# A margin behind the modelled landing of transfers, in the planner that orders the engines' queues of a two-layer decoder trunk

## The chip, the cores and the metric

One NeuronCore of one Trainium2 chip runs the kernel; the other cores idle. The metric is the device time of one execution in microseconds (us), and less is better.

## The reference

The input x is 256 positions by 2048 channels, float32, and passes through two layers. What each layer computes, cut to what matters here:

```python
h = rms_norm(x, mix_norm[l])
proj = h @ w_in[l]                       # 2048 -> 1024 + 512 + 2048 + 4096
q, k, v, uv, gate_logits = split(proj)
branch_a = sliding_window_attention(q, k, v, sinks[l]) @ w_attn_branch[l]
branch_b = chunked_sgu(gelu(uv), w_spatial[l], ...) @ w_sgu_branch[l]
x = x + (gates_a * branch_a + gates_b * branch_b) @ w_out[l]
h2 = rms_norm(x, ffn_norm[l])
x = x + (silu(h2 @ w_gate[l]) * (h2 @ w_up[l])) @ w_down[l]     # 2048 -> 5632 -> 2048
```

All is float32, and nearly all of the work is matrix products of the 256 positions with some 470 MB of weights, each weight read once.

## The kernel before

**Products.** A float32 product is made of three single-pass products: each operand is split into a high part and a low remainder. The weights arrive from HBM in tiles `raw` of 128x2x512 floats (512 KB). For each, ScalarE (ACT) writes the high part `whi` (line 520) and VectorE (DVE) the remainder `wlo` (line 521); TensorE (PE) then runs whi·uh, wlo·uh and whi·ul (lines 617 and 618) into PSUM tiles `acc`. The activations' parts are `uh` and `ul`. `raw` has 5 buffers (and four single ones, `k11` to `k22`), `whi` and `wlo` 4 each.

**Paired columns.** Where two 512-column blocks are computed together, a part of the product uses a seven-product scheme. Its entries P1 to P7 take differences of weight tiles, made in place on VectorE (`raw<-raw,raw`, line 506), and of activations (`sums`, split into `sh` and `sl`). In the middle of a pair, partial sums are saved and added (`kept`, lines 644 and 647) and put back into PSUM (`acc<-kept`, lines 645 and 650). P4 starts to write the PSUM tile that the second `kept` of line 647 reads, so PE waits there for that `kept`.

**Activations for the next product.** A result (a chunk of x after the residual, `hid`, a merged branch) is transposed in two steps: VectorE transposes 32x32 blocks into `box` (line 691), and 16 small DMAs, issued by POOL or SP, gather them into `tt` (line 697). ScalarE then reads `tt` and writes `uh` (line 716, or 720 where a norm's scale is applied) or a whole copy `flat` (line 761), and VectorE writes `ul` (lines 717 and 725).

**What sets the order.** PE's instructions stand in the order in which the program writes them. The queues of the other four (DVE, ACT, POOL, SP) are ordered by a planner (`in_order`) that runs while the kernel is built. `works` finds dependencies; `count_back` gives each instruction a due time from PE's order and a table of costs; `play` then plays the program forward by modelled costs. Whenever an engine is free, `play` gives it, of the instructions that are ready at that modelled time, the one that is due first. A transfer's modelled end is a queue of service times plus 1550 to 3100 ns, and the transfer's readers become ready then. The order that comes out is fixed: each engine takes its instructions in turn, and one that must wait holds up all behind it. The lines of `play` at which the change takes effect:

```python
            for u in w.users:
                if (todo[u].engine == w.engine and not w.dma) == (kind == 2):
                    release(u, t + (LATE if w.dma and kind == 1 else 0))
```

Here `w` is an instruction that has just ended in the model, `w.dma` tells that it is a transfer, and `release` makes the reader `u` ready.

Of the kernel before, what the change touches and what calls it, by code (L numbers as in the profile page):

```python
# [17 lines left out]
COST_PE = {"psg": 500, "po": 450, "psc": 400}  # L18
TABLES = {"Exp": 0, "Gelu_apprx_tanh": 11, "Silu": 18}
SWITCH = 4000  # L20
LATE = 0
EARLY = 40000
SPARE = 30000

# [213 lines left out]
def play(todo, users, homes):  # L238
# [9 lines left out]
    def release(k, at):  # L248
        left[k] -= 1
        ready[k] = max(ready[k], at, todo[k].due - EARLY)  # L250
        if not left[k]:
            waiting[todo[k].engine].append(k)
            heappush(events, (ready[k], 0, k))
# [10 lines left out]
    while events:  # L264
        t, kind, k = heappop(events)
        w = todo[k]
        if kind:
# [3 lines that stand above are left out]
        if kind == 1:  # L271
# [1116 lines left out]
```

## Time and profile before

| | us |
|---|---|
| runs of the kernel before (median of 3) | 2458.6 (2449.66 to 2458.63) |
| the profiled execution's own time | 2451.39 |
| its span, first to last instruction | 2449.7 |
| PE busy | 2417.1 (99%) |
| DVE busy | 2106.4 (86%) |
| ACT busy | 1543.6 (63%) |
| mean granted TensorE clock | 0.998 |

In the profile's views L506 is line 506 of the kernel, `out<-in` names the tiles that an instruction writes and reads, and x6 counts equal instructions in a row. In rows of the timeline the two numbers ahead are the start and the length in us, and the bracket gives the engine's idle time before the instruction and what ended it. PE's matmuls overlap: one of 512 columns is shown as 390 ns long, while in steady work the next starts 227 ns after it.

### The profile page before, as it was taken

The numbers are of one execution on the slowest core, as the hardware profiler recorded it, in microseconds if no ns is written. First come the engines' busy times: TensorE is split into PE (matmuls) and PEld (weight loads), VectorE is DVE, ScalarE is ACT, GpSimd is POOL, SyncE is SP. The second block draws the span as 40 slices with busy tenths as digits, with TensorE's granted clock in tenths as the row PEclk, the third lists the DMA queues.
The fourth block names the chain that finished last, engine by engine and source line by source line (L and its number), as shares of the span: only waits on it lengthen the run. The fifth ranks groups of instructions, "written<-read, shape, count | busy, mean of one in ns | idle before, by whom it ended". The sixth has DMA issues, their size and how long they took to land.

```text
span 2449.7 us, 31107 instructions
## 1 busy us (share of the span) xinstructions
PE 2417.1 (99%) x10692; PEld 1973.3 (81%) x10692; DVE 2106.4 (86%) x2409; ACT 1543.6 (63%) x1936; POOL 319.3 (13%) x573
## 2 busy tenths in 40 slices
PE   9999999989999999999999999999999999999999
PEld 7877888868887888888788778887788888887887
DVE  7789777978999898789887987878889999998898
ACT  6477555555666666666665775555666666666665
POOL 1100001122110011002301000011311101110110
PEclk9999999999999999999999999999999999999999
DMA  7855787677578767866767557767776786678664
GB/s 250 259 165 163 190 214 222 225 226 247 168 250 238 214 189 223 263 201 197 246 224 244 173 173 192 207 210 247 228 229 204 221 259 201 201 234 244 203 219 145
DMA packets 287375, 527.17 MB, mean 215 GB/s; under 512 B 28464, under 2 KB 40336, under 8 KB 287216
## 3 DMA queue, kind: packets, MB, share of 16 engines
q1 hardware_dynamic: 263056, 486.36, 64.3%
q0 software_dynamic: 23840, 38.56, 6.1%
q8 instruction: 83, 1.36, 0.2%
q14 instruction: 76, 0.62, 0.1%
q10 hardware_dynamic: 320, 0.27, 0.0%
HBM read 483.66 MB, written 16.78 MB: 204 GB/s over the span
## 4 chain that ended last, share of the span: by engine, by line
PE 56%; DVE 7%; DMA 6%; issue 3%; ACT 1%; POOL 1%; SPq 0%; ACTq 0%; DVEq 0%; POOLq 0%
PE acc L617 37%; PE acc L618 18%; DVE wlo L521 4%; DMA tt<-box 2%; DMA raw<-in_w_down_dram 2%; ACT whi L520 1%; DVE raw L506 1%; DMA raw<-in_w_up_dram 1%; POOL tt L697 1%; DMA raw<-in_w_out_dram 0%; DMA held_x<-part 0%; DVE box L691 0%; PE psc L1061 0%; DVE hid L1327 0%; DMA held_x<-x 0%
## 5 line engine op out<-in xcount | busy, mean ns | idle before, releaser
L520 ACT ACTIVATE whi<-raw 128x1024 fp32r<-128x1024 f32 (+1 forms) x1116 | 1173.4, 1058 | 675.2 <-PE acc L618 530.8
L521 DVE TENSOR_TENSOR wlo<-raw,whi 128x1024 fp32r<-128x1024 f32 (+1 forms) x1117 | 1337.9, 1217 | 241.7 <-ACT whi L520 234.9
L617 PE MATMUL acc<-wlo,uh 128*128 128x512 f32 x2854 | 1116.9, 391 | 17.5 <-DVE kept L647 11.0
L617 PE MATMUL acc<-whi,uh 128*128 128x512 f32 x2854 | 1118.9, 392 | 0.1
L618 PE MATMUL acc<-whi,ul 128*128 128x512 f32 x2854 | 1113.7, 390 | 0.0
L617 PEld LDWEIGHTS acc<-wlo,uh 128*128 128x128 f32 x2854 | 537.2, 188 | 140.2 <-DVE wlo L521 15.4
L617 PEld LDWEIGHTS acc<-whi,uh 128*128 128x128 f32 x2854 | 537.3, 188 | 117.5 <-issue 3.4
L618 PEld LDWEIGHTS acc<-whi,ul 128*128 128x128 f32 x2854 | 537.2, 188 | 112.5 <-DVE ul L725 0.8
L697 POOL DMA_DIRECT2D tt<-box x464 | 228.9, 500 | 1207.4 <-DVE box L691 456.0
L506 DVE TENSOR_TENSOR raw<-raw,raw 128x1024 f32<-128x1024 f32 x292 | 355.2, 1222 | 21.5 <-DMA raw<-in_w_up_dram 8.6
L617 PE MATMUL acc<-wlo,sh 128*128 128x512 f32 x584 | 228.4, 391 | 4.7 <-DVE wlo L521 4.7
L617 PE MATMUL acc<-whi,sh 128*128 128x512 f32 x584 | 228.4, 391 | 1.4 <-ACT acc L645 1.4
L618 PE MATMUL acc<-whi,sl 128*128 128x512 f32 x584 | 227.4, 389 | 0.0
L617 PEld LDWEIGHTS acc<-wlo,sh 128*128 128x128 f32 x584 | 109.6, 188 | 30.3 <-DVE wlo L521 7.4
L617 PEld LDWEIGHTS acc<-whi,sh 128*128 128x128 f32 x584 | 109.6, 188 | 26.5 <-ACT acc L645 1.8
L618 PEld LDWEIGHTS acc<-whi,sl 128*128 128x128 f32 x584 | 109.6, 188 | 22.7
L650 ACT ACTIVATE acc<-kept 128x512 f32<-128x512 f32 x102 | 60.7, 595 | 35.8 <-DVE kept L647 28.0
L647 DVE TENSOR_TENSOR kept<-acc,kept 128x512 f32<-128x512 f32 x102 | 69.7, 683 | 1.2 <-PE acc L618 1.2
L1212 POOL DMA_DIRECT2D held_x<-part x32 | 27.5, 858 | 294.4 <-ACT part L1211 294.4
L716 ACT ACTIVATE uh<-tt 128x512 fp32r<-128x512 f32 x42 | 24.8, 624 | 39.8 <-DMA tt<-box 27.8
L717 DVE TENSOR_TENSOR ul<-tt,uh 128x512 fp32r<-128x512 f32 x42 | 27.8, 687 | 23.3 <-ACT uh L716 20.9
L589 POOL TENSOR_TENSOR rv<-ve,neg_half 128x4 f32<-128x4 f32 x8 | 10.8, 1344 | 256.4 <-DVE ve L1155 256.4
(149 smaller groups left out, 934.0 us busy)
## 6 DMA issues: line engine op xcount, KB each, us to landing
raw<-in_w_in_dram SPq DMA_DIRECT2D x239, 512.0 KB, 4.8
raw<-in_w_gate_dram SPq DMA_DIRECT2D x176, 512.0 KB, 4.6
raw<-in_w_up_dram SPq DMA_DIRECT2D x176, 512.0 KB, 5.0
raw<-in_w_down_dram SPq DMA_DIRECT2D x176, 512.0 KB, 5.2
raw<-in_w_out_dram SPq DMA_DIRECT2D x64, 512.0 KB, 6.0
raw<-in_w_attn_branch_dram SPq DMA_DIRECT2D x64, 256.0 KB, 5.3
raw<-in_w_sgu_branch_dram SPq DMA_DIRECT2D x32, 512.0 KB, 5.0
tt<-box POOLq DMA_DIRECT2D x464, 32.0 KB, 4.7
```

Source lines behind the costliest of these rows:

```text
L506: nc.vector.tensor_tensor(out=self.raws[d], in0=self.raws[x], in1=self.raws[y], op=ALU.subtract)
L520: nc.scalar.activation(hi[:, i, :], raw[:, i, :], AF.Copy)
L521: nc.vector.tensor_tensor(out=lo[:, i, :], in0=raw[:, i, :], in1=hi[:, i, :].bitcast(F32), op=ALU.subtract)
L589: nc.gpsimd.tensor_tensor(out=dst, in0=src, in1=neg_half[:, :n], op=ALU.pow)
L617: nc.tensor.matmul(ps, a, part[:, kk, :], start=first and kk + n == 0, stop=False, skip_group_check=True)
L618: nc.tensor.matmul(ps, b, hi[:, kk, :], start=False, stop=kk == 1, skip_group_check=True)
L647: nc.vector.tensor_tensor(out=p.kept[int(tag == "P7")], in0=a[1], in1=p.kept[1], op=ALU.add)
L650: nc.scalar.activation(ps, p.kept[t], AF.Copy)
L697: q.dma_start(dst[j * B:(j + 1) * B, i], box[i * B:(i + 1) * B, j])
L716: nc.scalar.activation(h, s_, AF.Copy)
L717: nc.vector.tensor_tensor(out=l, in0=s_, in1=h.bitcast(F32), op=ALU.subtract)
L1212: nc.gpsimd.dma_start(held_x[j][:, t, :], part, accum_op=ALU.add)
```

## The change

The planner's constant `LATE` goes from 0 to 3000 (ns). In `play`, a reader of a transfer becomes ready 3000 ns after the transfer's modelled landing instead of at it. Transfers are still modelled to land, and their buffers to be free, as before; no instruction is added, removed or altered, PE's order is the same, and the waits are those that the data need.

```diff
-LATE = 0
+LATE = 3000
```

The other queues come out in another order at many places, by a few positions each. Three places follow. Names carry the program's numbers here.

ScalarE's queue at the end of the first layer's output projection, where the FFN's activations are built (`uh_913` from the gathered `tt_915`) between splits of weights:

```order
 L520 ACTIVATE whi_941_4795<-raw_907_4612 128x1024
 L650 ACTIVATE acc_960_4909<-kept_928_4729 128x512
-L720 ACTIVATE uh_913_4662<-tt_915_4664,vcols_199 128x256 x3
 L520 ACTIVATE whi_944_4819<-raw_935_4769 128x1024
-L720 ACTIVATE uh_913_4662<-tt_915_4664,vcols_199 128x256
 L520 ACTIVATE whi_947_4832<-raw_938_4783 128x1024
+L720 ACTIVATE uh_913_4662<-tt_915_4664,vcols_199 128x256 x2
 L650 ACTIVATE acc_961_4910<-kept_929_4730 128x512
+L720 ACTIVATE uh_913_4662<-tt_915_4664,vcols_199 128x256 x2
```

The four readers of `tt_915` stood ahead of the weight splits `whi_944` and `whi_947`, and now stand behind them.

VectorE's queue at the same place; `kept_929` is the one that PE waits for before P4:

```order
 L521 TENSOR_TENSOR wlo_942_4796<-raw_907_4612,whi_941_4795 128x1024
-L725 SCALAR_TENSOR_TENSOR ul_914_4663<-tt_915_4664,vcols_199,uh_913_4662 128x128 x6
+L521 TENSOR_TENSOR wlo_945_4820<-raw_935_4769,whi_944_4819 128x1024
 L647 TENSOR_TENSOR kept_929_4730<-acc_920_4673,kept_929_4730 128x512
-L521 TENSOR_TENSOR wlo_945_4820<-raw_935_4769,whi_944_4819 128x1024
 L521 TENSOR_TENSOR wlo_948_4833<-raw_938_4783,whi_947_4832 128x1024
 L1219 SCALAR_TENSOR_TENSOR x_826_4205<-acc_887_4506,x_826_4205 128x512
+L725 SCALAR_TENSOR_TENSOR ul_914_4663<-tt_915_4664,vcols_199,uh_913_4662 128x128
```

`kept_929` stood behind six pieces of `ul_914`, which need the gathered `tt_915`; it now stands behind one `wlo` alone.

VectorE's queue at the start of the first layer's down projection (`raw_1248` and the others are weight tiles or differences of them):

```order
 L521 TENSOR_TENSOR wlo_1271_6475<-raw_1194_6085,whi_1270_6474 128x1024
-L506 TENSOR_TENSOR raw_1248_6365<-raw_1266_6453,raw_1248_6365 128x1024
 L521 TENSOR_TENSOR wlo_1276_6492<-raw_1243_6343,whi_1275_6491 128x1024
 L521 TENSOR_TENSOR wlo_1278_6502<-raw_1247_6363,whi_1277_6501 128x1024
+L506 TENSOR_TENSOR raw_1247_6363<-raw_1266_6453,raw_1247_6363 128x1024
 L521 TENSOR_TENSOR wlo_1280_6514<-raw_1269_6472,whi_1279_6513 128x1024
+L521 TENSOR_TENSOR wlo_1282_6525<-raw_1274_6489,whi_1281_6524 128x1024
 L506 TENSOR_TENSOR raw_1243_6343<-raw_1260_6429,raw_1243_6343 128x1024
```

The first reader of the transfer into `raw_1266` stood ahead of `wlo_1276` and `wlo_1278`, which read other tiles. Now both come first, another reader of `raw_1266` follows, and the difference `raw_1248` stands 15 places further back, three places ahead of the remainder that reads it.

## The prediction

> **What bounds the kernel now.** I read the page first, then PE's table of waits, then the windows in which PE runs fewest matmuls, and last the timeline of each engine there.
>
> ```profile
> span 2449.7 us, 31107 instructions
> PE 2417.1 (99%) x10692; PEld 1973.3 (81%) x10692; DVE 2106.4 (86%) x2409; ACT 1543.6 (63%) x1936; POOL 319.3 (13%) x573
> ```
>
> PE is busy nearly throughout, and the change takes no matmul away. Only PE's pauses can be won. In windows of 100 us (columns: busy us and count of PE, PEld, DVE, ACT, POOL; granted clock; DMA share, GB/s) they show as missing matmuls:
>
> ```profile
> 300.00:400.00 100.00, 100.00 (x442) 82.65 (x441) 81.50 (x85) 59.81 (x69) 0.00 (x0) 1.00 0.77 214
> 500.00:600.00 100.00, 94.11 (x398) 76.25 (x397) 81.47 (x109) 59.55 (x80) 25.80 (x49) 0.97 0.72 227
> 600.00:700.00 100.00, 98.65 (x435) 81.38 (x434) 93.83 (x111) 65.06 (x74) 23.33 (x48) 1.00 0.70 211
> 700.00:800.00 100.00, 98.15 (x433) 80.78 (x432) 91.15 (x86) 66.03 (x73) 9.10 (x14) 1.00 0.77 236
> 1700.00:1800.00 100.00, 93.58 (x400) 75.61 (x399) 81.32 (x106) 61.57 (x87) 27.00 (x54) 0.98 0.71 222
> ```
>
> A full stretch holds 442, one per 226 ns. The two weak ones lack 44 and 42, together 86 x 0.226 = 19.4 us; they are the passages from the mixer to the FFN in layers 0 and 1. The rest is thin: 7 and 9 missing in the other two rows. PE's own waits, and the two that concern the splits' buffers:
>
> ```profile
> PE acc L617 <- DVE kept L647: 11.0, 5, 4.5
> PE acc L617 <- DVE wlo L521: 10.9, 19, 1.8
> PE acc L617 <- ACT acc L645: 1.4, 1, 1.4
> ACT whi L520 <- PE acc L618: 530.8, 600, 2.6
> SPq L496 <- DVE wlo L521: 1369.8, 576, 9.4
> ```
>
> So PE pauses 25 times for 23.3 us. The fourth row says that ACT's splits wait for PE to free a buffer 600 times: usually they run as far ahead as four buffers let them. PE pauses where something holds ACT or DVE up, and the timeline shows what.
>
> **The change part by part.** It adds and removes no instruction, so its whole cost or gain lies in who stands behind whom. A pause of PE costs its idle time plus 0.16 us (a matmul is shown 390 ns long, and the next is due 227 ns after its start).
>
> Term 1, the end of each output projection (the first two order pieces above). Layer 0, then layer 1:
>
> ```profile
> 543.64 1.30 ACT L720 ACTIVATE uh<-tt,vcols 128x256 fp32r<-128x256 f32 x3 [5.71 <-DMA tt<-box]
> 544.18 1.67 DVE L725 SCALAR_TENSOR_TENSOR ul<-tt,vcols,uh 128x128 fp32r<-128x128 f32 x6 [4.62 <-ACT uh L720]
> 545.76 0.68 DVE L647 TENSOR_TENSOR kept<-acc,kept 128x512 f32<-128x512 f32 x1
> 546.50 0.80 PE L617 MATMUL acc<-wlo,uh 128*128 128x512 f32 x1 [4.50 <-DVE kept L647]
> 1761.00 1.31 ACT L720 ACTIVATE uh<-tt,vcols 128x256 fp32r<-128x256 f32 x3 [4.61 <-DMA tt<-box]
> 1763.86 0.50 PE L617 MATMUL acc<-wlo,uh 128*128 128x512 f32 x1 [3.45 <-DVE kept L647]
> ```
>
> ACT stands still for 5.71 us because the reader of `tt` is next in its queue; DVE for 4.62 us behind the pieces of `ul`; and `kept`, which needs neither, is behind them. In the new order `kept` has one `wlo` ahead of it. Its split can begin when ACT's queue reaches it, at about 537.9 (543.64 less 5.71); split (1.04) plus `wlo` (1.2, DVE being free from 544.18 - 4.62 = 539.56) plus `kept` (0.68) end near 541.5, and PE's pause began near 542.0 (546.50 - 4.50). That its weights and a buffer are there by 537.9 no row shows; were they 2 us late, a pause of 1.5 us would be left. I take the pause as gone: 4.50 + 0.16 and 3.45 + 0.16 = 8.3 us. What is late next: the pieces of `ul`, some 9 us of DVE work further back, which also starts 4.6 us earlier; PE takes this unit up only after the passage's remaining entries, so I cost it at nothing.
>
> The clock goes with it. Windows just after those two pauses, and after a shorter one:
>
> ```profile
> 545.70:552.50 6.80, 6.00 (x14) 4.74 (x15) 6.76 (x9) 5.38 (x10) 0.43 (x1) 0.50 0.51 152
> 1764.30:1767.70 3.40, 3.40 (x10) 2.64 (x9) 3.37 (x5) 2.76 (x6) 0.00 (x0) 0.51 0.44 119
> 741.50:748.50 7.00, 7.00 (x32) 5.78 (x31) 7.00 (x8) 5.01 (x7) 0.00 (x0) 1.00 0.46 120
> ```
>
> At full clock they would hold 30 and 15 matmuls; 16 and 5 are missing, 21 x 0.226 = 4.7 us. Idle 1.85 us (below) leaves the clock at 1.00, idle 3.45 us halves it. If a pause were only shortened to something between, these rows leave up to 4.7 us open; I take the pauses as gone, so the clock's 4.7 us as won. The Trainium skill, "TensorE: Matmul & The Clock Gate", "What's actually happening", puts the drop at an idle window of about 3.4 us: by it even a pause cut to 2.5 us would win the whole of the clock's share, where the rows alone would let me count between none and all. That the window runs freely, as it says, no row here can show.
>
> Term 2, the middle of the output projection, the same pattern with `flat`:
>
> ```profile
> 492.97 1.31 ACT L761 ACTIVATE flat<-tt,vcols 128x256 f32<-128x256 f32 x3 [2.85 <-DMA tt<-box]
> 495.26 1.23 DVE L521 TENSOR_TENSOR wlo<-raw,whi 128x1024 fp32r<-128x1024 f32 x1 [3.71 <-ACT whi L520]
> 497.14 0.50 PE L617 MATMUL acc<-wlo,uh 128*128 128x512 f32 x1 [1.37 <-DVE kept L647]
> 1715.52 0.50 PE L617 MATMUL acc<-wlo,uh 128*128 128x512 f32 x1 [1.55 <-DVE kept L647]
> ```
>
> In the new order two `whi` go ahead of all four `flat`. DVE's 3.71 us of idle time shrinks by about ACT's 2.85, more than PE's pause. Gain 1.37 + 1.55 + 0.32 = 3.2 us.
>
> Term 3, a third stop of ACT for `tt`:
>
> ```profile
> 519.02 0.51 ACT L720 ACTIVATE uh<-tt,vcols 128x256 fp32r<-128x256 f32 x1 [6.84 <-DMA tt<-box]
> 521.80 0.50 PE L617 MATMUL acc<-wlo,uh 128*128 128x512 f32 x1 [0.76 <-DVE wlo L521]
> 1740.25 0.50 PE L617 MATMUL acc<-wlo,uh 128*128 128x512 f32 x1 [0.77 <-DVE wlo L521]
> ```
>
> Two `whi` go ahead of that `uh`: 0.76 + 0.77 + 0.32 = 1.9 us.
>
> Term 4, differences of weights that wait for a transfer (the third order piece, its twin in layer 1, and one in the last down projection):
>
> ```profile
> 738.70 1.22 DVE L506 TENSOR_TENSOR raw<-raw,raw 128x1024 f32<-128x1024 f32 x1 [2.74 <-DMA raw<-in_w_down_dram]
> 741.12 0.50 PE L617 MATMUL acc<-wlo,sh 128*128 128x512 f32 x1 [1.85 <-DVE wlo L521]
> 1952.75 1.23 DVE L506 TENSOR_TENSOR raw<-raw,raw 128x1024 f32<-128x1024 f32 x1 [2.08 <-DMA raw<-in_w_down_dram]
> 1955.17 0.50 PE L617 MATMUL acc<-wlo,sh 128*128 128x512 f32 x1 [1.19 <-DVE wlo L521]
> 2248.05 1.23 DVE L506 TENSOR_TENSOR raw<-raw,raw 128x1024 f32<-128x1024 f32 x1 [2.31 <-DMA raw<-in_w_up_dram]
> 2250.46 0.50 PE L617 MATMUL acc<-wlo,sh 128*128 128x512 f32 x1 [1.37 <-DVE wlo L521]
> ```
>
> The two `wlo` behind each had their `whi`; now they run in DVE's idle time. Gain 1.85 + 1.19 + 1.37 + 0.48 = 4.9 us.
>
> The other waits for `wlo`: 10.9 us less the 5.9 in terms 3 and 4 is 5.0 in 14 pauses, with 14 x 0.16 some 7.2 us. At about half of them, by the two orders, the `wlo` that PE waits for moves ahead by one difference (1.22 us) and at the others by nothing. I take 3.6, between 0 and 7.2. One large pause stays, since its rows stand in the same order in both:
>
> ```profile
> 661.80 1.16 ACT L716 ACTIVATE uh<-tt 128x512 fp32r<-128x512 f32 x2 [4.01 <-DMA tt<-box]
> 666.58 0.50 PE L617 MATMUL acc<-whi,sh 128*128 128x512 f32 x1 [1.35 <-ACT acc L645]
> ```
>
> What comes back: the change also puts 47 of the 292 differences more than 1 us of DVE work later (and 31 earlier). Where a split follows its difference at once, the split now starts one or two `wlo` (1.2 us each) later. No row shows a pause from that. Its bounds are 0, as four filled buffers suggest, and 23 us, half a microsecond for each of the 47. I take 6, nearer the lower end, because the moved ones mostly yield to a `wlo` that PE needs sooner, and because SP's and POOL's queues hardly change: the transfers start when their buffers come free, no later than before.
>
> Sum: 8.3 + 4.7 + 3.2 + 1.9 + 4.9 + 3.6 - 6 = 20.6 us. Against the profiled execution's own 2451.4 us (span 2449.7) that is 2431 us. The median of the runs is 7.2 us above this execution; I don't know what made them differ and don't carry it over, but let the range cover it.
>
> **The rivals.** The line between a change and none is 0.5%, 12 us, about what a measurement of this kernel can tell.
>
> A: the waits move on. ACT no longer stops for `tt` ahead of two `whi`, but ahead of the third; a difference no longer holds two `wlo` up, but the next. For it speaks DVE's 91 to 94% in the FFN windows, which leaves little to catch up with; against it, that the freed time lies ahead of the pause, and that at term 1 the transfer has landed by 543.64, before a third split is due. Then half of the 23.0 us of terms 1 to 4 comes back and the 3.6 isn't won: 11.5 - 6 = 5.5 us, 2446.
>
> B: the transfers themselves are what PE lacks. 576 issues on SP wait for a `wlo` to free a buffer (row above), so a late landing would be a matter of how many buffers there are, no order would help, and the time would stay at 2451. Against it: at terms 1 and 4 the instructions held up needed nothing of the transfer that held them. The Trainium skill, "Perfetto Trace Analysis", "Optimization Strategy", says that the same gap repeating on the engine that should be saturated can mean too few buffers; the pauses here do repeat from layer to layer, but the rows name a queue's order as the cause.
>
> C: slower. The delayed differences reach PE. The place is every paired block of the FFN and the down projections; the price is 1.2 us, one `wlo`, for each of the 47, 56 us, against 26.6 won: 2481. It decides from 26.6 / 47 = 0.57 us per moved difference on. Against it, the 600 waits of ACT for PE: the splits mostly have time in hand.
>
> **How the numbers follow.** The main case (gain of 12 to 30 us) has 0.75; A 0.11, B 0.07, C 0.07 (0.06 slower by over 12 us, 0.01 within). Faster 0.75, same 0.19, slower 0.06. The main case alone runs from 2420 (all of 23.0 + 7.2, nothing back) to 2439. The range for 8 in 10 adds A, and the execution-to-execution difference above it: 2419 to 2449. The predicted time is the main case's, 2431.
>
> **What would show it.** Term 1: no PE wait for `kept` above 1 us near 540 and 1755, no window with the clock at 0.50 there, and 435 or more matmuls in the two weak windows. Term 2: no pause near 495 and 1710. Term 4: differences with no long idle time ahead of them and `wlo` just before. PE's waits in total fall from 23.3 us to under 10. The pause at 666 stays. I am wrong if PE has new waits for `wlo` right after differences, or if `uh` and `ul` of the FFN's first units come to be what PE waits for near 560 and 1780.

## The result, and the profile after

| | before | after |
|---|---|---|
| runs, median us | 2456.7 (2449.66 to 2458.63, 4 runs) | 2413.9 (2413.39 to 2417.52, 4 runs) |
| profiled execution's own time, us | 2451.4 | 2413.7 |
| its span, us | 2449.7 | 2412.0 |

The changed kernel is faster by 1.7%: the ratio is 0.9834, with a 95% interval of 0.9811 to 0.9857. Between the two profiled executions the span fell by 37.7 us. The prediction forecast 20.6 us and a time of 2431 us, and its range ended at 2419 us. So the direction held and the size did not. All the accounts below are made between the two spans.

The page of the changed kernel, in the same lines as before (all work is the same; only PE's share and the span move):

```profile
span 2412.0 us, 31137 instructions
PE 2402.3 (100%) x10692; PEld 1973.6 (82%) x10692; DVE 2109.8 (87%) x2409; ACT 1544.7 (64%) x1936; POOL 320.1 (13%) x573
```

PE's whole table of waits after (what it waited for: us in total, times, longest):

```profile
PE pt L734 <- DMA x<-in_x_dram: 1.9, 1, 1.9
PE acc L617 <- DVE wlo L521: 1.2, 3, 0.5
PE pwarm L569 <- DVE warm L564: 1.1, 1, 1.1
PE acc L617 <- ACT acc L645: 1.0, 1, 1.0
PE acc L618 <- DVE ul L725: 0.4, 1, 0.4
```

No wait for `kept` is left, and of 19 waits for `wlo` there are three. The rows for `x`, `pwarm` and `ul` (at 9.8 us) and one of the three `wlo` (17.6) belong to the start of the program, and `acc` is the one pause that was forecast to stay. The two other waits for `wlo`, at 897.0 and 2094.3, are new; the part on the prediction returns to them. The windows after, two of 100 us, and then the two places where the clock had been halved:

```profile
500.00:600.00 100.00, 100.00 (x443) 82.89 (x442) 91.11 (x116) 64.42 (x81) 29.99 (x60) 1.00 0.79 246
1700.00:1800.00 100.00, 100.00 (x443) 82.89 (x442) 90.90 (x116) 64.46 (x83) 26.99 (x55) 1.00 0.75 241
545.70:552.50 6.80, 6.80 (x32) 5.64 (x30) 4.23 (x6) 3.44 (x6) 1.34 (x2) 1.00 0.60 176
1764.30:1767.70 3.40, 3.40 (x17) 2.82 (x16) 3.37 (x4) 3.04 (x4) 0.00 (x0) 1.00 0.26 60
```

The two weak stretches of 398 and 400 matmuls now hold 443 each, as many as any. The timeline of the changed kernel at the end of the first layer's output projection (rows of DVE, ACT and PE, by start):

```profile
533.68 0.68 DVE L647 TENSOR_TENSOR kept<-acc,kept 128x512 f32<-128x512 f32 x1
533.76 0.90 ACT L720 ACTIVATE uh<-tt,vcols 128x256 fp32r<-128x256 f32 x2
535.27 0.39 PE L617 MATMUL acc<-wlo,uh 128*128 128x512 f32 x1
536.01 0.34 DVE L725 SCALAR_TENSOR_TENSOR ul<-tt,vcols,uh 128x128 fp32r<-128x128 f32 x1
```

The matmul at 535.27 is the one that stood at 546.50 before, behind 4.50 us of idle time. `kept` is now ahead of the pieces of `ul` and done at 534.36, 0.9 us before PE takes it up. Nor does ACT wait for `tt` any more: its row carries no bracket, so the gathered rows were there at 533.76. Over the whole program, ScalarE's waits that a transfer's landing ended fell from 127.8 to 58.3 us, and VectorE's from 22.1 to 6.6.

**Where the 37.7 us came from.** PE's order is the same in both kernels, and both traces hold all 10,314 matmuls of L617 and L618. So the nth of one can be set beside the nth of the other: the difference of their starts is the lead that the new kernel has won by then. The growth of the lead over a stretch (times of before) is the gain of that place. Each kernel is here one execution; experiment 3 shows that a place can differ by some 1 us between executions of the same order.

| place | stretches, us | forecast | measured |
|---|---|---|---|
| term 1 with its clock | 540 to 552.6, 1760 to 1768 | 13.0 | 12.9 |
| term 2 | 490 to 499, 1710 to 1718 | 3.2 | 3.5 |
| term 3 | 515 to 523.5, 1735 to 1742 | 1.9 | 2.7 |
| term 4 | 735 to 743, 1947 to 1957, 2240 to 2252 | 4.9 | 5.3 |
| right behind term 1 | 552.6 to 600, 1768 to 1800 | part of -6 | 0.1 |
| all the rest | | 3.6 and the rest of -6 | 13.2 |
| sum | | 20.6 | 37.7 |

The four terms brought 24.4 us where 23.0 were forecast. Of the miss of 17.1 us, 15.7 lie in the last two rows.

### The profile page after: what moved, and what is told of

The parts are those of the page before. It is cut to its first block, busy times and chain, and to the rows that moved or that the text cites. A ratio compares the mean times of both kernels' runs of the same rounds, so it can differ in the third digit from the quotient of the medians.

```text
span 2412.0 us, 31137 instructions
## 1 busy us (share of the span) xinstructions
PE 2402.3 (100%) x10692; PEld 1973.6 (82%) x10692; DVE 2109.8 (87%) x2409; ACT 1544.7 (64%) x1936; POOL 320.1 (13%) x573
## 4 chain that ended last, share of the span: by engine, by line
PE 70%; DVE 2%; DMA 1%; issue 0%; ACT 0%; SPq 0%; DVEq 0%; ACTq 0%
PE acc L617 46%; PE acc L618 23%; DVE wlo L521 1%; DMA raw<-in_w_up_dram 0%; DVE raw L506 0%; ACT whi L520 0%; PE psc L1061 0%; PE po L1110 0%; DMA raw<-in_w_down_dram 0%; DMA tt<-box 0%; PE psg L1190 0%; PE ppt L1095 0%; PE pt L734 0%; DVE ul L766 0%; DVE hid L1327 0%
## 5 line engine op out<-in xcount | busy, mean ns | idle before, releaser
L617 PE MATMUL acc<-whi,uh 128*128 128x512 f32 x2854 | 1117.7, 392 | 0.1
L617 PE MATMUL acc<-wlo,uh 128*128 128x512 f32 x2854 | 1113.5, 390 | 0.3 <-DVE wlo L521 0.2
L618 PE MATMUL acc<-whi,ul 128*128 128x512 f32 x2854 | 1113.0, 390 | 0.4 <-DVE ul L725 0.4
L617 PEld LDWEIGHTS acc<-whi,uh 128*128 128x128 f32 x2854 | 536.5, 188 | 115.8 <-issue 3.4
L617 PEld LDWEIGHTS acc<-wlo,uh 128*128 128x128 f32 x2854 | 536.6, 188 | 112.7 <-DVE wlo L521 2.7
L618 PEld LDWEIGHTS acc<-whi,ul 128*128 128x128 f32 x2854 | 536.6, 188 | 112.1 <-DVE ul L725 1.0
L617 PE MATMUL acc<-whi,sh 128*128 128x512 f32 x584 | 228.6, 391 | 1.0 <-ACT acc L645 1.0
L617 PE MATMUL acc<-wlo,sh 128*128 128x512 f32 x584 | 228.2, 391 | 1.0 <-DVE wlo L521 1.0
L618 PE MATMUL acc<-whi,sl 128*128 128x512 f32 x584 | 227.6, 390 | 0.0
L617 PEld LDWEIGHTS acc<-whi,sh 128*128 128x128 f32 x584 | 109.7, 188 | 26.1 <-issue 1.5
L617 PEld LDWEIGHTS acc<-wlo,sh 128*128 128x128 f32 x584 | 109.7, 188 | 24.9 <-DVE wlo L521 2.0
L618 PEld LDWEIGHTS acc<-whi,sl 128*128 128x128 f32 x584 | 109.7, 188 | 22.7
L644 ACT ACTIVATE kept<-acc 128x512 f32<-128x512 f32 x51 | 30.2, 593 | 30.7 <-PE acc L618 30.6
L1081 ACT ACTIVATE pr<-pr,negm 128x128 f32<-128x128 f32 x64 | 24.9, 391 | 17.1 <-DVE negm L1074 17.0
```

The source lines that it names most:

```text
L617: nc.tensor.matmul(ps, a, part[:, kk, :], start=first and kk + n == 0, stop=False, skip_group_check=True)
L618: nc.tensor.matmul(ps, b, hi[:, kk, :], start=False, stop=kk == 1, skip_group_check=True)
L644: nc.scalar.activation(p.kept[1], a[0], AF.Copy)
L1081: nc.scalar.activation(pr4[:, h, :], pr4[:, h, :], AF.Exp, bias=nm_[:, h:h + 1], accum_out=den[:, h:h + 1])
```

## The experiments

The theory: the planner's queues were wrong because its transfers land too early in its model. Every planned landing can be set beside the one in the trace of before. The weight transfers were modelled to land 3.59 us (median) after their issue and took 4.87 us; transfer by transfer they took 1.0 us (median) and at the ninth tenth 2.9 us longer than modelled. A reader placed by the modelled landing then blocks its queue for that long, with other work behind it. The rivals: (a) only the stage of term 1 counts, the rest is chance; (b) the transfers lack buffers; (c) any later reader gives the gain, whatever the landings do, or only one class of readers matters.

**1 and 2: each class of readers alone.** The margin is kept for readers of weights, then for readers of all other transfers (mostly the gathers `tt`).

```diff
-release(u, t + (LATE if w.dma and kind == 1 else 0))
+release(u, t + (LATE if w.dma and kind == 1 and w.outs[0][0].startswith("raw") else 0))
```

> The margin of 3000 ns for readers of weight tiles (raw) alone; readers of gathered activations keep a margin of 0, so at the ends of the output projections kept stands behind the six pieces of ul as before. Theory 1 (each pause belongs to one reader that heads a queue): the differences and splits of weights (term 4 and the small pauses, 4.9 + 7.2 us, and some 3 us of pauses too short for the table of waits) go, the pauses for kept (11.0 us with the halved clock behind them) stay: 13 to 16 us faster than before, profiled span 2434 to 2437, PE's waits for kept still about 10 us. Rival (the pauses hang together: once DVE and ACT have time in hand, all shrink): over 25 us faster, waits for kept under 4 us. Rival (delayed differences give time back): less than 8 us faster.

```diff
-release(u, t + (LATE if w.dma and kind == 1 else 0))
+release(u, t + (LATE if w.dma and kind == 1 and not w.outs[0][0].startswith("raw") else 0))
```

> The margin for all transfers but the weights (the gathers into tt and the rows of x), so kept goes ahead of the pieces of ul, while the first difference of a late weight tile still stands ahead of the two wlo. Theory 1: terms 1 to 3 go (8.3 + 4.7 + 3.2 + 1.9 us, and 3 us of PE's transposes that waited for x): 18 to 22 us faster, span 2428 to 2432; PE's waits for wlo stay near 10 us in some 17 pauses. If the parts add up, the gains of this run and of the one with the weights alone make about 37 us together. Rival (they hang together): the two sum to well over 45 us.

Weights alone: 2442.6 us, ratio 0.9966 (0.9946 to 0.9986), 8.1 us of the span. The others alone: 2426.4 us, ratio 0.9893 (0.9868 to 0.9919), 26.2 us. PE's waits, first with the margin for weights alone, then for the others alone:

```profile
PE acc L617 <- DVE kept L647: 9.1, 5, 4.3
PE acc L617 <- DVE wlo L521: 5.7, 9, 1.0
```

```profile
PE acc L617 <- DVE wlo L521: 4.4, 9, 1.2
PE acc L617 <- DVE kept L647: 0.3, 1, 0.3
```

By the lead, the weights' margin wins all of term 4 (5.3 us), 1.7 of term 2's 3.5 and 1.5 of term 1's 12.9. The gathers' margin wins terms 1 to 3 whole (19.1 us) and 2.7 of term 4. Each class relieves its own waits for landings: with the weights' margin VectorE's fall to 8.6 us and ScalarE's stay at 126.5, with the others' ScalarE's fall to 60.9 and VectorE's stay at 25.0. Both expectations were off, the first too high by 5 to 8 us, the second too low by 4 to 8. The two gains add up to 34.3 us; 3.4 are left for the two together, less than the runs of either kernel spread over (13 and 6 us).

**3: the stage of term 1 alone.** The margin holds only for the gathers of the FFN's first activations, `tt_915` and its twin.

```diff
-release(u, t + (LATE if w.dma and kind == 1 else 0))
+release(u, t + (LATE if w.dma and kind == 1 and w.outs[0][0].startswith(("tt_915", "tt_2997")) else 0))
```

> The margin of 3000 ns for the readers of two gathers alone, the one of each layer at the end of its output projection (the first two order pieces of the document): term 1 by itself. All other queues stand as before but for some 30 rows. Theory 1: the two pauses for kept (4.50 and 3.45 us idle) and the two stretches of halved clock go, and PE comes into the FFN 8.3 + 4.7 = 13.0 us earlier: span 2435 to 2439, waits for kept about 3 us in 3, none for ul of these units. Rival (the time comes back at the next stop, the prediction's A): the two pauses go, others grow, span 2442 to 2450.

2441.7 us, ratio 0.9952 (0.9936 to 0.9968), 7.5 us of the span. Its waits:

```profile
PE acc L617 <- DVE wlo L521: 13.2, 25, 1.6
PE acc L617 <- DVE kept L647: 0.5, 2, 0.3
```

The long pauses for `kept` are gone and term 1 gains its full 12.9 us, but 6.0 us are lost right behind it (47 and 32 us long), in new waits for `wlo`, and 4.8 in the rest. The places of terms 2 to 4 show 5.4 us of gain, which is not all the order's: in the first layer all queues of this kernel are those of before up to 537 us, and still the lead loses 1.1 us at 419 and wins 1.15 at term 2. From one execution to the next, a place where a queue stops for a landing can differ by that much. The prediction's rival A, waits that move on, is real when one place is mended by itself. Rival (a) of the theory falls: the gain needs the other places too.

**4 and 5: smaller margins.** `LATE` is 1000, then 2000.

> A margin of 1000 ns for all. The planner's own landings against the traced ones (929 weight transfers): modelled 3.59 us at the median, measured 4.87; the measured one is later by 1.0 us at the median and by 2.9 us at the ninth tenth. Theory 2 (the margin works by covering the planner's error): 1000 covers half of the transfers, so clearly less than the whole gain: 15 to 28 us faster, span 2422 to 2435, with some waits for wlo behind differences left. Rival (any margin reorders enough): the same as with 3000, span 2410 to 2415.

> LATE is 2000. Theory 1 (the gain follows the share of landings whose error the margin covers; beside the trace of before, a margin of 1 us covers 46% of the errors, 2 us 76%, 3 us 91%, and 1000 brought 20.4 us of the span's 37.7): 2000 brings about 30 us, span 2416 to 2424, with a few waits for wlo left, under 5 us in all. Rival (the places of the queues jump at a few thresholds, and 3000 happens to be the first value past all of them): 2000 gives what 1000 gave, 2426 to 2432. A third way (everything is won by 2000 already): 2410 to 2415.

1000: 2429.4 us, ratio 0.9911 (0.988 to 0.9942). 2000: 2421.6 us, ratio 0.9862 (0.9844 to 0.9881). With 1000 the timeline behind term 1 shows what came back:

```profile
557.87 0.51 ACT L720 ACTIVATE uh<-tt,vcols 128x256 fp32r<-128x256 f32 x1 [5.61 <-DMA tt<-box]
558.41 0.61 DVE L725 SCALAR_TENSOR_TENSOR ul<-tt,vcols,uh 128x128 fp32r<-128x128 f32 x2 [2.13 <-ACT uh L720]
569.28 0.50 PE L617 MATMUL acc<-wlo,uh 128*128 128x512 f32 x1 [0.74 <-DVE wlo L521]
```

ACT stops 5.61 us for the next gather, and DVE runs out of slack 11 us later. The queue has moved its stop from one `tt` to the next, as the prediction's rival A says. At 2000 waits for `wlo` are down to half:

```profile
PE acc L617 <- DVE wlo L521: 4.7, 9, 1.7
```

**6 and 7: larger margins.** `LATE` is 5000, then 9000.

> LATE is 5000, which covers 99% of the landings' errors. Theory 1 (past the errors a margin has nothing left to win, and readers set too late begin to hold up PE): span 2412 to 2435, with waits for whi or wlo coming back, over 5 us in all, since 9000 cost 117 us against 3000. Rival (the loss comes only where the margin outruns the buffers or PE's own run-ahead, well past 5000): 2409 to 2414 and no such wait.

> A margin of 9000 ns, three times what the planner's error needs. Theory 2: nothing more to win; readers are now put behind work that is due later than they are, so PE waits for units (ul) or for differences: 2415 to 2440, slower than with 3000. Rival (later is always better while four buffers are filled): 2408 to 2413.

5000: 2443.4 us, ratio 0.9952 (0.9936 to 0.9967). 9000: 2531.8 us, ratio 1.0321 (1.0291 to 1.0351), with PE waiting 37 us for splits:

```profile
PE acc L617 <- ACT whi L520: 37.1, 14, 4.8
```

At 5000 the waits are small; the 13 for `whi`, each with one for `wlo` behind it, stand at places that are mostly some 42.5 us apart:

```profile
PE acc L617 <- DVE wlo L521: 12.2, 17, 1.3
PE acc L617 <- ACT whi L520: 9.0, 13, 1.6
```

One such place, in rows of DVE, ACT and PE with 5000, and the same differences and splits with 3000 below:

```profile
900.11 2.35 DVE L506 TENSOR_TENSOR raw<-raw,raw 128x1024 f32<-128x1024 f32 x2
901.36 3.90 ACT L520 ACTIVATE whi<-raw 128x1024 fp32r<-128x1024 f32 x4 [0.34 <-DVE raw L506]
902.47 0.50 PE L617 MATMUL acc<-whi,sh 128*128 128x512 f32 x1 [1.33 <-ACT whi L520]
904.25 0.50 PE L617 MATMUL acc<-wlo,sh 128*128 128x512 f32 x1 [1.28 <-DVE wlo L521]
```

```profile
893.13 2.35 DVE L506 TENSOR_TENSOR raw<-raw,raw 128x1024 f32<-128x1024 f32 x2
894.38 3.90 ACT L520 ACTIVATE whi<-raw 128x1024 fp32r<-128x1024 f32 x4 [0.91 <-DVE raw L506]
```

With 5000, DVE and ACT have just done other work (`sl`, `hid`), and the differences are so late that PE comes to them first. That is the prediction's rival C, at a larger margin. Both losses were larger than I expected: the span at 5000 lies 7 us above the range, at 9000 90 us. Of the five margins 3000 is the best. By the lead, every one of them wins terms 1 to 4 whole; they differ in the rest:

| margin, us | landings whose error it covers | span, us | won, us | terms 1 to 4 | right behind term 1 | the rest | ACT's and DVE's waits for landings, us |
|---|---|---|---|---|---|---|---|
| 1 | 46% | 2429.3 | 20.4 | 24.4 | -5.8 | 1.8 | 114.3 and 15.1 |
| 2 | 76% | 2420.3 | 29.4 | 24.4 | -4.7 | 9.7 | 81.0 and 9.8 |
| 3 | 91% | 2412.0 | 37.7 | 24.4 | 0.1 | 13.2 | 58.3 and 6.6 |
| 5 | 99% | 2441.6 | 8.1 | 24.4 | 0.1 | -16.4 | 39.7 and 8.4 |
| 9 | at least 99% | 2529.7 | -80.0 | 24.4 | -7.5 | -97.0 | 39.4 and 20.2 |

The second column counts, over all 1776 transfers of before, those that took from issue to landing no more than the margin longer than modelled; without a margin it is 10%. Up to 3 us the gain follows it (54%, 78% and 100% of 37.7), and the waits for landings fall with it from 127.8 and 22.1. The median error alone, 1 us, is worth about half of the gain; the other half is room for the scatter. At 5 and 9 us ScalarE waits for landings still less, but PE now waits for ScalarE and VectorE.

**8: the model's landings.** `LATE` is 0, and the planner's fixed latencies are 3000 larger, so the landings themselves are modelled later.

```diff
-self.dma = serve, (2200 if far else 1550) + (900 if self.engine == POOL and size > 40000 else 0)
+self.dma = serve, (5200 if far else 4550) + (900 if self.engine == POOL and size > 40000 else 0)
```

> No margin, but the planner's own latency of a transfer raised by 3000 ns (2200 to 5200 and 1550 to 4550), so its landing, its buffers' release and the due time of its issue move too. Theory 2 (what counts is that readers are planned by a landing that the chip keeps): nearly the gain of the margin, span 2411 to 2422. Rival (the margin works because it leaves the transfers' own plan alone): transfers are issued otherwise and the gain is under 20 us, span over 2430.

2416.3 us, ratio 0.9853 (0.9833 to 0.9873), 35.9 us of the span, with four waits for `wlo` left:

```profile
PE acc L617 <- DVE wlo L521: 2.2, 4, 1.0
```

Nearly the whole gain comes without the margin, from later landings in the model. This fits an order that had followed landings which were too early. By itself it doesn't separate such landings from rival (c), since the readers move back by the same 3000 ns. Against (c) stand the waits for landings in the table above, and the two larger margins, where later readers lose. A model with the right median and scatter of each transfer was not tried.

**9: a sixth weight buffer.** `LATE` is 0, and one buffer moves to the weights.

```diff
-big = pool("big", 31)
-wraw = pool("wraw", 5)
+big = pool("big", 30)
+wraw = pool("wraw", 6)
```

> No margin, but six buffers for weight tiles instead of five (and 30 slots for activations instead of 31): the prediction's rival B. If too few buffers made the landings late, the pauses for wlo go and the time falls by 8 us or more, to 2444 or less. Theory 1 (a queue's order): transfers start a buffer earlier, so a part of the waits of differences for their tile shrinks, but ACT's stops for gathers stay: pauses for kept still 8 to 11 us, span 2438 to 2452.

2447.9 us, ratio 0.9982 (0.9967 to 0.9998), 1.6 us of the span. The pauses for `kept` are two instead of five, with nearly the same total:

```profile
PE acc L617 <- DVE kept L647: 10.2, 2, 5.5
```

By the lead, terms 2 and 3 are won here (6.2 us) and 2.2 of term 4, but term 1 loses 2.9, its second pause being 5.5 us long, and the rest loses 4.0. The queues' order changes with the buffers too, so what the buffer does by itself is not separated. ScalarE's waits for landings stay at 114.1 us and VectorE's rise to 28.2. So one more buffer doesn't bring the gain, and rival (b) falls as the account of it; the prediction's rival B, by which no order would help, fell with the result. B's reading had been taken from the Trainium skill, "Perfetto Trace Analysis", "Optimization Strategy", where a repeated gap can mean too few buffers; this run speaks against it here, as the buffer brought 1.6 us and the order 37.7.

**10 and 11: which class the large margin hurts.** Weights at 9000 and the others at 3000, then the others at 9000 and weights at 3000.

```diff
-release(u, t + (LATE if w.dma and kind == 1 else 0))
+release(u, t + ((9000 if w.outs[0][0].startswith("raw") else LATE) if w.dma and kind == 1 else 0))
```

> 9000 ns for the readers of weights, 3000 for all others. With 9000 for all, the time rose to 2531 and PE waited 37.1 us for whi in 14 pauses. Theory 3 (a difference that is planned too late holds up the split, the first of a paired block): this run has the same 14 pauses or nearly, span 2490 to 2530. Rival (late units did it): under 2430, with PE's waits for whi gone.

```diff
-release(u, t + (LATE if w.dma and kind == 1 else 0))
+release(u, t + ((LATE if w.outs[0][0].startswith("raw") else 9000) if w.dma and kind == 1 else 0))
```

> The margin is 9000 for the readers of all transfers but the weights', and 3000 for the weights'. Theory 1 (the loss at 9000 comes from the weights' readers, on which every matmul waits in turn; the other transfers are few and their readers' results are needed much later): 2410 to 2425. Rival (a margin of 9000 is too long for the gathers too, whose activations the FFN's first matmuls need): waits for uh or ul come up, 10 us or more, 2430 to 2460.

The first took 2539.2 us in one run (span 2537.5), above the expected range and with 19 pauses for `whi`: the weights' readers alone make the whole loss of the 9000 for all (span 2529.7). The second took 2446.8 us, ratio 0.997 (0.9951 to 0.999), 33.1 us more in the span than with 3000 for all. I had expected next to nothing there, and was wrong. Their waits:

```profile
PE acc L617 <- ACT whi L520: 46.0, 19, 5.5
```

```profile
PE acc L617 <- ACT uh L720: 11.6, 3, 6.5
PE acc L617 <- ACT uh L716: 3.6, 2, 2.6
```

The gathers have little room too: at 9 us the FFN's first activations come behind the matmuls that need them.

**12: one engine's readers alone.** The margin holds for readers on ScalarE.

```diff
-release(u, t + (LATE if w.dma and kind == 1 else 0))
+release(u, t + (LATE if w.dma and kind == 1 and todo[u].engine == ACT else 0))
```

> The margin stands for readers on ScalarE alone (differences and the other readers on VectorE become ready at the modelled landing, as before). Theory 1 (the waits at the ends of the output projections come from ul, which needs uh and so moves with ScalarE's readers, while the differences of the down projections are VectorE's own): the waits for kept go, the waits for wlo at the first and second down projection stay, 4 to 8 us of them; span 2422 to 2434. Rival (a late transfer hurts only through VectorE's queue, which is the busier of the two): at most 8 us are won, 2440 to 2448.

2426.3 us, ratio 0.9884 (0.9866 to 0.9902), 26.0 us of the span, and the waits for `wlo` that remain:

```profile
PE acc L617 <- DVE wlo L521: 6.9, 13, 1.6
```

Terms 1 to 3 are won whole through ACT's queue, of term 4 only 2.2 of 5.3 us. `kept` stands in VectorE's queue, but it was late because the pieces of `ul` ahead of it waited for `uh`, and `uh` for `tt`. The other 11.7 us need the margin on the readers of the other engines as well; 3.1 of them are term 4, VectorE's differences.

## Why the prediction was wrong in size

Right were the mechanism and its four terms: readers of late transfers held up work behind them, and with them moved, the pauses and the halved clock went, place by place, at 24.4 us for 23.0. All that was said to show it came: no wait for `kept`, 443 matmuls in both weak windows, the clock at 1.00, under 10 us of waits, and the pause at 666 in its place (at 652 now, 1.0 us). Rivals A and B did not come about at this margin, and C only in two small pauses. (The main case's lower end is 2421, not 2420: 23.0 + 7.2 off 2451.4.) Four steps failed, all to the same side; the two large ones are terms of the sum that were mis-sized, -6 that came to -1.5 and 3.6 that came to 8.3.

- "What comes back", taken as 6 us, came to 1.5. In two places, one in each layer, the change puts a difference behind one more `wlo` and a piece of `sums`, and PE waits for the first remainder that reads it, at 897.01 (row below) and 2094.25. That is the sign named for being wrong; each costs 0.75 us. At the other 45 moved differences no pause is left. A loss of 6 us was the price of a smaller margin, and in another place: 1000 and 2000 lose 5.8 and 4.7 us right behind term 1. At 3000 the next stop for `tt` there is gone as well. I weighed only the differences, and not that the gathers' own start might move. The trace's rows for the tile `tt`, from 520 to 550 before and 510 to 540 after (shortest, median and longest issue in ns, then start of the first and last), show that it did:

```profile
L697 POOL DMA_DIRECT2D tt<-box x16: 498/498/509, 529.4 to 538.3; - x16
```

```profile
L697 POOL DMA_DIRECT2D tt<-box x16: 496/497/507, 520.6 to 527.9; - x16
```

 The first of the 16 is issued 8.8 us earlier and the last 10.4, while PE is 6.4 and 6.6 us ahead at these points. So against the matmuls they start 2.4 to 3.8 us earlier: the work that feeds them was held up in the same queues (VectorE's last `box` ahead of them starts at 519.57 instead of 528.38). For these gathers the sentence that transfers start "no later than before" was true and too weak.

- "About half" of the other waits for `wlo`, taken as 3.6 us: 13 of these 14 pauses, with 4.8 us of idle time, are gone; the one at the start of the program stays. With 0.27 us of overhead each (next point) that is 8.3 us. I had counted only pauses at which the awaited `wlo` itself moved ahead in VectorE's queue. By the two orders that is so at seven of the 13. At four others only its `whi` moved ahead, in ScalarE's queue, and at two, near 445 and 1664, neither did; there the `wlo` ends 1.3 and 1.5 us ahead of PE now, with time won further up the queues. These two are gone as well with 2000, with 5000 and with either class alone. Of the table's last row, weights alone and gathers alone win -0.7 and 4.3 us, both together 13.2, in one execution each.

- A pause's overhead of 0.16 us was too small. Rows of PE in the changed kernel:

```profile
896.14 0.39 PE L617 MATMUL acc<-whi,sh 128*128 128x512 f32 x1
897.01 0.50 PE L617 MATMUL acc<-wlo,sh 128*128 128x512 f32 x1 [0.48 <-DVE wlo L521]
897.35 0.39 PE L618 MATMUL acc<-whi,sl 128*128 128x512 f32 x1
```

 The first matmul after a pause is 0.50 us long, not 0.39, and the next starts 0.34 later, not 0.227. From 896.14 to 897.35 are 1.21 us for two steps of 0.227: the pause cost 0.76, its idle 0.48 and 0.27 more. The pauses before show the same 0.27. Over the nine pauses of terms 1 to 4 the missing 0.11 makes 1.0 us, most of the 1.4 between 23.0 and 24.4.

- What PE's table of waits for L617 does not show was left out. One is PE's transposes (L734); a wait and the group's row before, then the group's row after:

```profile
PE pt L734 <- DVE x L1219: 1.4, 1, 1.4
...
L734 PE MATMUL pt<-ident,x 128*128 128x128 f32 x48 | 7.7, 302 | 3.6 <-DMA x<-in_x_dram 2.1 <-DVE x L1219 1.4
```

```profile
L734 PE MATMUL pt<-ident,x 128*128 128x128 f32 x48 | 6.6, 278 | 1.9 <-DMA x<-in_x_dram 1.9
```

 Busy and idle time together fell from 11.3 to 8.5, 2.8 us. The other is pauses so short that the overlap of matmuls hides them. Outside the stretches of halved clock, intervals between the ends of two matmuls that are 0.1 to 0.37 us over the steady 0.227 number 11 before and one after. Two of the 11 lie in term 3's stretches, where they explain its excess; the other nine cost 1.6 us more than the one after.

For the table's last row, 8.3 - 1.5 + 2.8 + 1.6 = 11.2 us of 13.2 are found. By the lead, 1.1 more stand at the fifth wait for `kept` (near 1206), at the pause that stays and behind the last matmul; 0.9 is spread over intervals too short to name.

The medians fell by 42.8 us, 5.1 more than the profiled spans, since the profiled execution of before was 5.3 us under its median. The runs of before spread over 9 us there and over 11.6 us (2447.0 to 2458.7) beside the last experiments, those of after over 4. That an order which waits for landings passes their scatter on would fit: the kernels with 2000 and more for all readers, and the one with later modelled landings, spread over 0.8 to 4.7 us, the one with 1000 over 12.4. No run was made to test it, and it stays open.

## What to carry to other kernels

Where a fixed order is planned by modelled landings, compare the model's landings with the trace's and try a margin for the readers of about the ninth tenth of the error (here 3 us, the best of five): a queue that stops for a late transfer stops all that stands behind it, while a reader that is somewhat late uses slack. The margin has an upper end, where readers arrive behind the bound engine (here between 3 and 5 us), so try values on both sides. When many small pauses of one cause are mended together, more of them may go than a sum place by place says; mended in one place alone, as in experiment 3, the wait moved to the next.

## What the runs showed of the hardware

Landings under this kernel's load are scattered, and later than its planner's model. The page's part on transfers, before (KB each, median us from issue to landing):

```profile
raw<-in_w_out_dram SPq DMA_DIRECT2D x64, 512.0 KB, 6.0
tt<-box POOLq DMA_DIRECT2D x464, 32.0 KB, 4.7
```

Of all 929 transfers into `raw` (66 of them of 256 KB) a tenth lands within 3.70 us and nine tenths within 7.32, at a mean of 215 GB/s of all transfers. The Trainium skill, "DMA: Bandwidth & Descriptors", "Anatomy of one DMA — SWDGE (gpsimd) path", gives a fixed 2.0 us plus the bytes at 436 GB/s, which I work out as an estimate of 3.2 us for 512 KB. The medians of this trace for 512 KB into `raw`, from 4.6 to 6.0 us, lie well above that. They are no test of that figure, since SP issues these transfers, and the kernel moves much else beside them.

The clock halves by where a pause falls, not by its length alone. In the run with gathers at 9000, PE's rows at one longer pause and then in both layers at the same place, and the windows just behind each:

```profile
574.06 0.50 PE L617 MATMUL acc<-whi,uh 128*128 128x512 f32 x1 [2.54 <-ACT uh L720]
787.20 0.50 PE L617 MATMUL acc<-whi,sh 128*128 128x512 f32 x1 [1.63 <-ACT whi L520]
788.46 0.50 PE L617 MATMUL acc<-wlo,sh 128*128 128x512 f32 x1 [0.76 <-DVE wlo L521]
1999.37 0.50 PE L617 MATMUL acc<-whi,sh 128*128 128x512 f32 x1 [1.63 <-ACT whi L520]
2000.64 0.50 PE L617 MATMUL acc<-wlo,sh 128*128 128x512 f32 x1 [0.76 <-DVE wlo L521]
```

```profile
574.70:578.70 4.00, 4.00 (x12) 3.15 (x12) 2.90 (x8) 0.51 (x2) 0.00 (x0) 0.57 0.03 1
788.50:793.00 4.50, 4.50 (x20) 3.76 (x21) 4.50 (x5) 3.90 (x5) 0.00 (x0) 1.00 0.35 54
2001.60:2005.10 3.50, 3.50 (x11) 2.75 (x10) 3.50 (x4) 2.00 (x3) 0.00 (x0) 0.54 0.25 45
```

The same two pauses, 2.4 us of idle time within 2.9 us, leave the clock at 1.00 in one layer and halve it in the other. The clock's changes in this trace fall on a fixed grid: its four halvings between 575 and 2002 are 617.8, 593.9 and 215.0 us apart, which is 181, 174 and 63 times 3.413 us. The Trainium skill, "TensorE: Matmul & The Clock Gate", "What's actually happening", says that the window of 3.4 us runs freely, and this grid agrees. Its idle window, as I read it in the prediction, these rows do not bear out: 2.4 us of idle time, with matmuls between, were enough, and so was one pause of 2.54. So the prediction's sentence that a pause cut to 2.5 us would by that rule save the clock's whole share does not hold in every phase. What share of a window must be idle, no run here shows.
